# Where the twelve weight buffers and the moving operands of a float32r kernel start in their SBUF rows

## The chip, the core and the metric

The kernel runs on one core of a Trainium2 chip. The metric is the device time of one execution in microseconds (us). An interval between two matmuls is given in nanoseconds (ns).

## What is computed

Two transformer blocks work on one sequence of 256 tokens of width 1024, in float32. The first block mixes with gated spatial products, decaying ("forgetting") attention and attention on a memory, and ends in a feed-forward layer. The second block has two layers. Each is a gated feed-forward layer, an attention (sliding window in the first layer, latent attention in the second), and another gated feed-forward layer. Cut to what carries the time:

```python
f = jnp.square(jax.nn.relu(h @ w_ff1[l])) @ w_ff2[l]            # first block
...
def swiglu(h, wg, wu, wd):
    return (jax.nn.silu(h @ wg) * (h @ wu)) @ wd
...
x = x + 0.5 * swiglu(rmsnorm_2(x, ffn_norm1[i]), ffn1_wg[i], ffn1_wu[i], ffn1_wd[i])
x = x + sliding_window_attention(...)    # layer 0; latent_attention in layer 1
x = x + 0.5 * swiglu(rmsnorm_2(x, ffn_norm2[i]), ffn2_wg[i], ffn2_wu[i], ffn2_wd[i])
```

The feed-forward layers of the second block have 2816 inner columns, that of the first 4096. Each weight is read once; 208.71 MB are read from HBM in all.

## The kernel before

**Products in three passes.** A float32 product is made from float32r halves: every weight and every activation is split into a high part and a low part, and high·high, high·low and low·high are summed in PSUM. `mm_t` (lines 131 to 139) does this for one tile of the transposed result. The weight is the stationary operand (128 columns of it are loaded for each matmul), the activation the moving one (256 columns, the tokens):

```python
pe.matmul(ps, lhsT=h[:, c:c + m], rhs=x[0][k], start=s0, stop=False)     # line 137
pe.matmul(ps, lhsT=h[:, c:c + m], rhs=x[1][k], start=False, stop=False)  # line 138
pe.matmul(ps, lhsT=lo[:, c:c + m], rhs=x[0][k], start=False, stop=s1)    # line 139
```

`mm_n` (lines 141 to 149) makes the untransposed result of a few products: there the weight is the moving operand (256 to 512 columns) and the activation the stationary one.

**The weight stream.** The class `Stream` brings weights in transfers of up to 2048 columns into three `raw` buffers. It cuts each into parts of up to 1024 columns. For a part, ScalarE casts the high half into a `wh` buffer (line 100) and VectorE, in a few places GpSimd, subtracts it to get the low half in a `wl` buffer (line 110). There are six `wh` and six `wl` buffers, taken in turn, so twelve in all. A part of 1024 columns feeds 24 matmuls of `mm_t`. The order of the work is written out by hand (`manual_schedule`), engine by engine.

**The moving operands.** `xh` and `xl` (lines 154 and 155) are the halves of the normed input, eight tiles each. They are the moving operand of all projections from the input of a layer: queries, keys, the gate and up products. `ah` and `al` are the halves of the inner activation of a feed-forward layer and move through the down products. `oh` and `ol` are those of the attention outputs, `mh` and `ml` those of the memory. Each such tile is 256 float32r columns, which is 1024 bytes of a row (the part of a tile that lies in one partition).

**Places in the row.** The pools are laid one behind the other in the order in which they are opened: constants (`cst`), weights (`wp`), residual and normed tiles (`res`), temporaries (`tp`, `sm`), then the pools of each stage. Each tile starts at a multiple of 32 bytes. The constants come to a length that is no multiple of 512, and so everything behind them up to the stage pools starts at the same odd place. In the built program, by first byte in the row:

| tiles | before | remainder by 512 | changed | remainder by 512 |
|---|---|---|---|---|
| `raw`, 3 buffers | 24,928 on | 352 | 17,536 on | 128 |
| `wh` | 49,504 to 69,984 | 352, all six | 42,112 on, every 8,256 | 128, 192, 256, 320, 384, 448 |
| `wl` | 74,080 to 94,560 | 352, all six | 46,240 on, every 8,256 | 160, 224, 288, 352, 416, 480 |
| `xh`, `xl` | 106,848 to 122,208 | 352 | 99,840 to 115,200 | 0 |
| `ah`, `al`, `oh`, `ol`, `mh`, `ml`, `ch`, `cl` | 138,240 and beyond | 0 | 138,752 and beyond | 0 |

The 128-column slices of a weight buffer that the matmuls load lie 512 bytes apart, so all slices of a buffer have the remainder of its start.

Of the kernel before, what the change touches and what calls it, by code (L numbers as in the profile page):

```python
# [9 lines left out]
F32 = mybir.dt.float32  # L10
F32R = mybir.dt.float32r
BF16 = mybir.dt.bfloat16
I32 = mybir.dt.int32
# [4 lines left out]
P = 128  # L18
T = 256
# [4 lines left out]
CHUNK_COLS = 2048  # L24
PART = 1024
DN_CUT = 6
GAINS = ["norm_pre_mix", "norm_post_mix", "norm_pre_ffn", "norm_post_ffn", "norm_mem"]
# [8 lines left out]
N_COLS = 101  # L36
# [14 lines left out]
def block_kernel(ctx: ExitStack, tc: tile.TileContext, a: dict, out: bass.AP, upto: int = 99):  # L51
    nc = tc.nc
    pool = lambda name, bufs, **kw: ctx.enter_context(tc.tile_pool(name=name, bufs=bufs, **kw))
    cst = pool("cst", 1)
    wp = pool("wp", 1)
    res = pool("res", 1)
    tp = pool("tp", 2)
    sm = pool("sm", 1)
    psp = pool("psp", 8, space=bass.MemoryType.PSUM)
# [3 lines left out]
    def bank():  # L63
        return psp.tile([P, 512], F32, tag="ps", name="ps")

    # weight stream -------------------------------------------------------
    order = []
    RAW, HL, AHEAD = 3, 6, 4

    class Stream:  # L70
        """Weights come in transfers of up to CHUNK_COLS columns, each cut into parts; a part is
        split into float32r halves whose sum is the float32 weight."""

# [17 lines left out]
        def split(self, eng=dve):  # L91
            i = self.ns
            while len(self.parts) <= i and self.nd < len(order):
                self.dma()
            if i >= len(self.parts):
                return False
            t, n, last = self.parts[i]
            h = wp.tile([P, PART], F32R, tag="wh", bufs=HL, name=f"wh{i}")
            lo = wp.tile([P, PART], F32R, tag="wl", bufs=HL, name=f"wl{i}")
            act.copy(h[:, :n], t)  # L100
            self.hl[i] = (h, lo)
            self.ns += 1
            self.low(eng)
            self.late = (lo[:, :n], t, h[:, :n], last)
            return True
# [18 lines left out]
        def fill(self):  # L124
            """As many parts as there is room for, the low part of the last still to come."""
            while self.ns < self.ng + HL and self.split(gp):
                pass

    ws = Stream()

    # products ------------------------------------------------------------
    def mm_t(ps, w, off, n, x, kts, first, last, m=P):
# [17 lines left out]

    # constants -----------------------------------------------------------
    ctx.enter_context(tc.manual_schedule())
# [3 lines left out]
    X = (xh, xl)  # L156
    cols = cst.tile([P, N_COLS], F32, name="cols")
    kon = cst.tile([P, 3 * P], F32, name="kon")
    kmask = cst.tile([P, 768], F32, name="kmask")
    rows = cst.tile([P, N_ROWS], F32, name="rows")  # L160
    posr = cst.tile([P, T], I32, name="posr")
    posc = cst.tile([P, 64], I32, name="posc")
    posn = cst.tile([P, 2], I32, name="posn")
    relb = cst.tile([P, 2, 16], F32, name="relb")
    mhalf = cst.tile([P, 32], F32, name="mhalf")
    gp.memset(mhalf, -0.5)
# [5 lines left out]
    def gcol(i, k):  # L172
        return cols[:, i * KT + k:i * KT + k + 1]
# [3 lines left out]

    # norms ---------------------------------------------------------------
    def rstd_pow(dst, src, n):
        gp.tensor_tensor(out=dst, in0=src, in1=mhalf[:, :n], op=ALU.pow)  # L180
# [61 lines left out]
    def prep(k, g, acc):  # L242
        """High part of a tile of the next normed input now, low part of the tile before."""
        act.activation(out=xh[k], in_=x[k], func=AF.Copy, scale=gcol(g, k))  # L244
        if acc is not None:
            add_sq(acc, k, x[k])
        prep_end()
        late.append((k, gcol(g, k)))
# [5 lines left out]

    # attention -----------------------------------------------------------
    def attn_exp(u):
# [68 lines left out]
    class Pipe:  # L325
        """Heads in flight: each step transposes the probabilities of the head two back, scores a
        new one, multiplies the values of the head three back, and goes on with the softmaxes."""

# [44 lines left out]

    # FFN of the second block ----------------------------------------------
    def ffn2(acc, gnext, extra=(), start=None, more=()):
# [52 lines left out]
    def out_proj_start(pipe, oh, ol, sets):  # L428
        """The first four tiles of an output projection, between the last steps of the heads."""
        ps, w, todo = [bank() for _ in range(4)], [], []  # L430
        seen = 0
        for ks in sets:
            for d in range(4):
                if not seen:
                    w.append(ws.get(max(0, HL - 2 - d)))
                mm_t(ps[d][:, :T], w[d], 0, P, (oh, ol), ks, not seen, False)
                pipe.done() or pipe.step()
            seen = 1
        while not pipe.done():
            pipe.step()  # L440
        return ps, w
# [28 lines left out]
    def y_evac(d, p, y, yacc, gi):  # L470
        """One tile of a post-normed sublayer: times its gain, and its squares."""
        if d == KT - 1:
            sq = tp.tile([P, T], F32, tag="sq", name="sq")
            act.activation(out=sq, in_=p, func=AF.Square)
        else:
            sq = None
            add_sq(yacc, d, p)
        act.activation(out=y[d], in_=p, func=AF.Copy, scale=gcol(gi, d))
        return sq

    # relative position bias: a threshold mask of the distances times the steps between buckets,
    # 8 groups of 4 keys a set, sets 0-3 for the first query tile
    rbd = cst.tile([P, 3, 64], BF16, name="rbd")

# [51 lines left out]

    # ======================================================================
    seq = [("w1f", 0, 4), ("w1q", 0, 6), ("w1k", 0, 2), ("w1m", 0, 1), ("w1v", 0, 2), ("w1u", 0, 3),
# [6 lines left out]
    for nm, i0, i1 in seq:  # L545
        for i in range(i0, i1):
            src = [a[nm][i, 0], a[nm][i, 1]] if len(a[nm].shape) == 4 else [a[nm][i]]
            for ap in src:
                n = ap.shape[-1]
                cut = cuts.get(nm) or ([DN_CUT * P, n] if nm.startswith("dn") else list(range(PART, n + 1, PART)))  # L550
                order.append((ap, cut))

# [1 line left out]
    warm_table(AF.Exp)  # L554
# [20 lines left out]
    with ExitStack() as es:  # L575
        mp = es.enter_context(tc.tile_pool(name="mix", bufs=1))
# [22 lines left out]

        # values and gates of the forgetting heads (natural)  # L600
        acc = new_acc()
# [16 lines left out]

        # queries and keys of the forgetting heads
        pq = [bank() for _ in range(3)]  # L620
# [98 lines left out]

        # queries of the memory heads, memory keys and values, with the forgetting heads in between  # L720
        for i in range(2):
# [22 lines left out]
        for tt in range(2):  # L744
            act.activation(out=vm[tt], in_=pv[tt][:, :T], func=AF.Copy, scale=rs_m[:, tt:tt + 1])
        # gating branch, with the memory heads in between
        pg = [bank(), bank()]
# [37 lines left out]
        for j in range(3):  # L785
# [10 lines left out]
            f = tp.tile([P, T], F32, tag="f", name="f")  # L796
            gp.tensor_tensor(out=f, in0=t, in1=uT[j], op=ALU.mult)
            split_plain(oh[j], ol[j], f)

        # output projection, post norm  # L800
        yacc = new_acc("macc")
# [18 lines left out]

# [1 line left out]
    with ExitStack() as es:  # L822
# [17 lines left out]
        for i in range(2):  # L840
            t = ft.tile([P, 2 * T], F32, tag="t", name="t")
            act.activation(out=t[:, :T], in_=p[i][:, :T], func=AF.Relu)
            f = ft.tile([P, 2 * T], F32, tag="f", name="f")
# [48 lines left out]

# [1 line left out]
    with ExitStack() as es:  # L894
# [34 lines left out]
        mp = es.enter_context(tc.tile_pool(name="swa", bufs=1))  # L929
# [7 lines left out]
        rq = mp.tile([P, KT, 2, 2], F32, name="rq")  # L937
        ga = mp.tile([P, 1], F32, name="ga")
        dve.scalar_tensor_tensor(out=ga, in0=cols[:, C_AQ:C_AQ + 1], scalar=0.125, in1=cols[:, C_AK:C_AK + 1],
# [91 lines left out]

# [1 line left out]
    tq = cst.tile([P, 2, 2, 32], F32, name="tq")  # L1033
    tk = cst.tile([P, 2, 2, 32], F32, name="tk")

# [32 lines left out]
    with ExitStack() as es:  # L1068
        mp = es.enter_context(tc.tile_pool(name="mla", bufs=1))
# [10 lines left out]
        ol = [mp.tile([P, T], F32R, name=f"ol{k}") for k in range(KT)]  # L1080
        gb = mp.tile([P, 1], F32, name="gb")
        rqb = mp.tile([P, 4, 2, 4], F32, name="rqb")
# [3 lines left out]
        warm_table(AF.Exp)  # L1086
        # latent projections, transposed: keys and values first
        w, w2 = ws.get(), ws.get()
# [230 lines left out]

# [1 line left out]
def _kp(w):  # L1321
# [136 lines left out]
```

## Time and profile before

| | |
|---|---|
| median of 3 runs | 1295.81 us (1295.09 to 1299.8) |
| span of the profiled execution | 1296.4 us (its own total is not recorded apart from the span) |
| TensorE matmul / weight load busy | 98% / 94% |
| VectorE / ScalarE / GpSimd busy | 65% / 51% / 15% |
| HBM read | 208.71 MB, 162 GB/s over the span |
| granted TensorE clock, mean | 0.989 |

Matmuls are pipelined: one shows a duration of 280 ns or so and the next starts long before it ends. What one costs is therefore the interval from its start to the start of the next, which the timeline and the counts of matmuls in a stretch show. "PE" rows are matmuls, "PEld" rows the loads of stationary operands; the load for the next matmul runs beside the current one.

### The profile page before, as it was taken

The page shows a single profiled execution, that of the slowest core. Times are in us where ns is not written, and L with a number is a line of the kernel's source. Part 1 is how long each engine was busy: PE and PEld are TensorE (multiplying, and loading weights), DVE is VectorE, ACT ScalarE, POOL GpSimd, SP SyncE. Part 2 cuts the span into 40 slices and gives each one's busy share as a digit, 9 for nine tenths or more (in the row PEclk, how much of TensorE's full clock was granted, in tenths as well). Part 3 has the DMA queues.
Part 4 walks back from the last instruction along what each step waited for, and adds up shares of the span by engine and source line. Part 5 has one row for each costly group of instructions (what it writes and reads, how often), then busy time and mean ns, then how long its engine had stood idle before and what let it go on. Part 6 is the DMA issues. An engine that isn't in the chain of part 4 may idle for free.

```text
span 1296.4 us, 24835 instructions
## 1 busy us (share of the span) xinstructions
PE 1270.1 (98%) x10316; PEld 1223.0 (94%) x10316; DVE 846.0 (65%) x1490; ACT 661.6 (51%) x1174; POOL 197.4 (15%) x192
## 2 busy tenths in 40 slices
PE   8999899999899999999999999999999999999998
PEld 7789899999799999977999999999999878999998
DVE  6886676654686666686766556666566786666553
ACT  5556455434344544565544444545444787444442
POOL 4424210110420001210300001100001451100000
PEclk9999899999899999999999999999999989999999
DMA  7534355565145545621555556545456412555453
GB/s 230 197 117 145 115 174 193 195 222 177 57 138 200 184 149 190 218 94 34 177 201 176 174 163 210 192 172 196 165 164 199 160 65 70 188 171 191 154 196 106
DMA packets 37265, 211.37 MB, mean 163 GB/s; under 512 B 4768, under 2 KB 8224, under 8 KB 18848
## 3 DMA queue, kind: packets, MB, share of 16 engines
q1 hardware_dynamic: 37152, 209.78, 47.8%
q8 instruction: 81, 1.33, 0.4%
q14 instruction: 32, 0.26, 0.1%
HBM read 208.71 MB, written 1.05 MB: 162 GB/s over the span
## 4 chain that ended last, share of the span: by engine, by line
PE 88%; DVE 7%; issue 2%; DMA 1%; ACT 1%; POOL 0%; SPq 0%; ACTq 0%; DVEq 0%; POOLq 0%
PE ps L137 26%; PE ps L138 26%; PE ps L139 26%; DVE wl L110 3%; PE ps L289 2%; PE ps L315 2%; PE ps L300 1%; PE ps L147 1%; PE ps L148 1%; PE ps L149 1%; DMA raw<-in_w1k 1%; PE ps L317 1%; DMA raw<-in_w1f 0%; DVE dg L226 0%; ACT wh L100 0%
## 5 line engine op out<-in xcount | busy, mean ns | idle before, releaser
L137 PE MATMUL ps<-xh,wh 128*128 128x256 f32 (+1 forms) x1848 | 529.6, 287 | 1.6 <-ACT xh L525 1.6
L138 PE MATMUL ps<-xl,wh 128*128 128x256 f32 (+1 forms) x1848 | 527.1, 285 | 1.4 <-DVE xl L532 0.9
L139 PE MATMUL ps<-xh,wl 128*128 128x256 f32 (+1 forms) x1848 | 525.7, 284 | 2.0 <-DVE wl L110 2.0
L110 DVE TENSOR_TENSOR wl<-raw,wh 128x1024 fp32r<-128x1024 f32 (+3 forms) x434 | 489.3, 1166 | 48.1 <-ACT wh L100 46.5
L100 ACT CAST wh<-raw 128x1024 fp32r<-128x1024 f32 (+4 forms) x436 | 400.2, 957 | 67.0 <-PE ps L138 28.6
L137 PEld LDWEIGHTS ps<-xh,wh 128*128 128x128 f32 (+1 forms) x1848 | 356.6, 193 | 5.3 <-issue 3.2
L138 PEld LDWEIGHTS ps<-xl,wh 128*128 128x128 f32 (+1 forms) x1848 | 356.5, 193 | 3.4 <-DVE xl L532 2.3
L139 PEld LDWEIGHTS ps<-xh,wl 128*128 128x128 f32 (+1 forms) x1848 | 356.8, 193 | 2.2 <-DVE wl L110 2.2
L137 PE MATMUL ps<-ah,wh 128*128 128x256 f32 x960 | 268.6, 280 | 0.0
L138 PE MATMUL ps<-al,wh 128*128 128x256 f32 x960 | 268.6, 280 | 0.0
L139 PE MATMUL ps<-ah,wl 128*128 128x256 f32 x960 | 268.5, 280 | 0.0
L137 PEld LDWEIGHTS ps<-ah,wh 128*128 128x128 f32 x960 | 180.5, 188 | 0.0
L138 PEld LDWEIGHTS ps<-al,wh 128*128 128x128 f32 x960 | 180.5, 188 | 0.0
L139 PEld LDWEIGHTS ps<-ah,wl 128*128 128x128 f32 x960 | 180.5, 188 | 0.0
L385 ACT ACTIVATE s<-t 128x256 f32<-128x256 f32 x88 | 36.8, 418 | 204.3 <-DVE t L383 204.3
L191 POOL TENSOR_TENSOR acc<-acc,sq 128x256 f32<-128x256 f32 x42 | 49.9, 1188 | 598.2 <-ACT sq L190 598.1
L383 DVE TENSOR_TENSOR t<-ps,rb 128x256 f32<-128x256 f32 x88 | 37.2, 423 | 85.4 <-PE ps L139 79.9
L205 DVE TENSOR_TENSOR al<-f,ah 128x256 fp32r<-128x256 f32 (+1 forms) x105 | 48.9, 466 | 52.8 <-ACT ah L204 52.8
L204 ACT CAST ah<-f 128x256 fp32r<-128x256 f32 (+1 forms) x105 | 45.9, 437 | 55.7 <-DVE f L387 43.1
L244 ACT ACTIVATE xh<-x,cols 128x256 fp32r<-128x256 f32 x40 | 20.4, 510 | 101.8 <-DVE x L420 94.7
L387 DVE TENSOR_TENSOR f<-ps,s 128x256 f32<-128x256 f32 x88 | 37.3, 424 | 47.4 <-ACT s L385 47.4
L419 DVE SCALAR_TENSOR_TENSOR t<-ps,rb 128x256 f32<-128x256 f32 x32 | 13.6, 424 | 77.1 <-PE ps L139 77.1
(285 smaller groups left out, 1322.8 us busy)
## 6 DMA issues: line engine op xcount, KB each, us to landing
raw<-in_gu SPq DMA_DIRECT2D x88, 1024.0 KB, 5.0
raw<-in_dn SPq DMA_DIRECT2D x64, 704.0 KB, 4.3
raw<-in_ff SPq DMA_DIRECT2D x32, 1024.0 KB, 4.9
raw<-in_w_out SPq DMA_DIRECT2D x4, 1024.0 KB, 4.9
raw<-in_aq SPq DMA_DIRECT2D x4, 1024.0 KB, 5.0
raw<-in_a_out SPq DMA_DIRECT2D x4, 1024.0 KB, 4.8
raw<-in_b_out SPq DMA_DIRECT2D x4, 1024.0 KB, 4.9
raw<-in_w1q SPq DMA_DIRECT2D x6, 512.0 KB, 3.9
```

The costliest lines, as they stand in the source:

```text
L100: act.copy(h[:, :n], t)
L110: eng.tensor_tensor(out=lo, in0=t, in1=h.bitcast(F32), op=ALU.subtract)
L137: pe.matmul(ps, lhsT=h[:, c:c + m], rhs=x[0][k], start=s0, stop=False)
L138: pe.matmul(ps, lhsT=h[:, c:c + m], rhs=x[1][k], start=False, stop=False)
L139: pe.matmul(ps, lhsT=lo[:, c:c + m], rhs=x[0][k], start=False, stop=s1)
L191: gp.tensor_tensor(out=acc, in0=acc, in1=sq, op=ALU.add)
L204: act.copy(h, src)
L205: dve.tensor_tensor(out=lo, in0=src, in1=h.bitcast(F32), op=ALU.subtract)
L289: pe.matmul(ps[:, o:o + n], lhsT=u["q"][:, i * P:i * P + P], rhs=u["k"][:, :n], start=True, stop=True)
L383: dve.tensor_tensor(out=t, in0=g, in1=rb, op=ALU.mult)
L385: act.activation(out=s, in_=t, func=AF.Silu)
L387: dve.tensor_tensor(out=f, in0=u, in1=s, op=ALU.mult)
```

## The change

The weight buffers get a tag of their own each, so that they are laid out `wh0, wl0, wh1, wl1, ...`, and each is 8 columns (32 bytes) longer than the 1024 that are used. A part still goes to buffer `i % HL`, the sixth part after it to the same one. The pools are reordered and a filler tile is added in such a way that `xh` and `xl`, and all pools behind, start at multiples of 512 bytes. Two 1-column tiles (`ga`, `gb`) become 32 columns wide with only the first used, and the rope tables `tq`, `tk` are placed with the other constants. The instructions of each engine, their order, their shapes and what each waits for are the same in both programs; only addresses differ.

```diff
+STAGGER = 8
...
-    cst = pool("cst", 1)
+    lead = pool("lead", 1)
     wp = pool("wp", 1)
     res = pool("res", 1)
     tp = pool("tp", 2)
+    cst = pool("cst", 1)
     sm = pool("sm", 1)
...
-            h = wp.tile([P, PART], F32R, tag="wh", bufs=HL, name=f"wh{i}")
-            lo = wp.tile([P, PART], F32R, tag="wl", bufs=HL, name=f"wl{i}")
+            h = wp.tile([P, PART + STAGGER], F32R, tag=f"wh{i % HL}", name=f"wh{i}")
+            lo = wp.tile([P, PART + STAGGER], F32R, tag=f"wl{i % HL}", name=f"wl{i}")
             act.copy(h[:, :n], t)
...
+    lead.tile([P, 32], F32, name="fill")
+    mhalf = lead.tile([P, 32], F32, name="mhalf")
+    rbd = lead.tile([P, 3, 64], BF16, name="rbd")
+    relb = lead.tile([P, 2, 16], F32, name="relb")
+    posc = lead.tile([P, 64], I32, name="posc")
     kon = cst.tile([P, 3 * P], F32, name="kon")
     kmask = cst.tile([P, 768], F32, name="kmask")
+    posr = cst.tile([P, T], I32, name="posr")
+    tq = cst.tile([P, 2, 2, 32], F32, name="tq")
+    tk = cst.tile([P, 2, 2, 32], F32, name="tk")
+    cols = cst.tile([P, N_COLS], F32, name="cols")
...
-        ga = mp.tile([P, 1], F32, name="ga")
+        ga = mp.tile([P, 32], F32, name="ga")[:, 0:1]
...
-        gb = mp.tile([P, 1], F32, name="gb")
+        gb = mp.tile([P, 32], F32, name="gb")[:, 0:1]
```

## Rows read from the trace of the kernel before

**Rows 1.** Page: span, busy time of each engine, granted clock in 40 slices.

```profile
span 1296.4 us, 24835 instructions
PE 1270.1 (98%) x10316; PEld 1223.0 (94%) x10316; DVE 846.0 (65%) x1490; ACT 661.6 (51%) x1174; POOL 197.4 (15%) x192
...
PEclk9999899999899999999999999999999989999999
```

**Rows 2.** Page: chain that ended last, share by engine.

```profile
PE 88%; DVE 7%; issue 2%; DMA 1%; ACT 1%; POOL 0%; SPq 0%; ACTq 0%; DVEq 0%; POOLq 0%
```

**Rows 3.** Groups by line: engine, operation, names, shapes, count | busy us, mean ns | idle before.

```profile
L138 PE MATMUL ps<-xl,wh 128*128 128x256 f32 (+1 forms) x1848 | 527.1, 285 | 1.4 <-DVE xl L532 0.9 <-DVE xl L253 0.5
L138 PE MATMUL ps<-al,wh 128*128 128x256 f32 x960 | 268.6, 280 | 0.0
L138 PE MATMUL ps<-ol,wh 128*128 128x256 f32 x192 | 53.8, 280 | 0.0
L138 PE MATMUL ps<-ml,wh 128*128 128x256 f32 x16 | 4.5, 280 | 0.0
L138 PEld LDWEIGHTS ps<-xl,wh 128*128 128x128 f32 (+1 forms) x1848 | 356.5, 193 | 3.4 <-DVE xl L532 2.3 <-DVE xl L253 0.9
L138 PEld LDWEIGHTS ps<-al,wh 128*128 128x128 f32 x960 | 180.5, 188 | 0.0
```

**Rows 4.** Timeline of PE, x products (640 us): start us, us, engine, line, operation.

```profile
640.07 0.28 PE L139 MATMUL ps<-xh,wl 128*128 128x256 f32 x1
...
676.07 0.28 PE L139 MATMUL ps<-xh,wl 128*128 128x256 f32 x1
```

**Rows 5.** Timeline of PE, down products (960 us).

```profile
960.04 0.28 PE L137 MATMUL ps<-ah,wh 128*128 128x256 f32 x1
...
995.24 0.28 PE L137 MATMUL ps<-ah,wh 128*128 128x256 f32 x1
```

**Rows 6.** Stretches: us, busy (count) of PE, PEld, DVE, ACT, POOL, clock, DMA.

```profile
640.00:680.00 40.00, 40.00 (x335) 40.00 (x335) 25.98 (x39) 19.90 (x30) 0.00 (x0) 1.00 0.51 168
960.00:1000.00 40.00, 40.00 (x343) 40.00 (x342) 26.15 (x37) 18.92 (x33) 6.04 (x5) 1.00 0.58 189
541.00:612.00 71.00, 71.00 (x479) 56.82 (x479) 49.82 (x180) 43.32 (x135) 10.68 (x10) 1.00 0.24 86
```

**Rows 7.** Timeline of PE, memory values (65 us): moving weight, stationary memory tile.

```profile
65.19 0.28 PE L147 MATMUL ps<-wh,mh 128*128 128x256 f32 x1
...
67.35 0.28 PE L147 MATMUL ps<-wh,mh 128*128 128x256 f32 x1
```

**Rows 8.** Timeline of PE, latent projection (1008 us): stationary loads of 32 columns.

```profile
1008.78 0.28 PE L138 MATMUL ps<-xl,wh 128*32 128x256 f32 x1
...
1010.48 0.28 PE L138 MATMUL ps<-xl,wh 128*32 128x256 f32 x1
```

**Rows 9.** Timeline of PE, 384 moving columns, stationary xh (90 us).

```profile
90.65 0.33 PE L147 MATMUL ps<-wh,xh 128*128 128x384 f32 x1
...
91.69 0.33 PE L147 MATMUL ps<-wh,xh 128*128 128x384 f32 x1
```

**Rows 10.** Timeline of PE, 384 moving columns, stationary ch (1022 us).

```profile
1022.59 0.34 PE L147 MATMUL ps<-wh,ch 128*128 128x384 f32 x1
...
1023.65 0.34 PE L147 MATMUL ps<-wh,ch 128*128 128x384 f32 x1
```

**Rows 11.** Weight stream: the cast, the subtraction, the landing of a transfer, SyncE's waits.

```profile
L110 DVE TENSOR_TENSOR wl<-raw,wh 128x1024 fp32r<-128x1024 f32 (+3 forms) x434 | 489.3, 1166 | 48.1 <-ACT wh L100 46.5 <-PE ps L138 1.1
L100 ACT CAST wh<-raw 128x1024 fp32r<-128x1024 f32 (+4 forms) x436 | 400.2, 957 | 67.0 <-PE ps L138 28.6 <-DMA raw<-in_dn 15.8 <-DMA raw<-in_w1q 7.1
raw<-in_gu SPq DMA_DIRECT2D x88, 1024.0 KB, 5.0
SPq L86 <- DVE wl L110: 984.9, 202, 22.3
```

More of the change, by code (lines that the diff above doesn't have):

```diff
@@ L156, in block_kernel @@
     X = (xh, xl)
-    cols = cst.tile([P, N_COLS], F32, name="cols")
+    lead.tile([P, 32], F32, name="fill")
[3 more added lines that the diff above has]
+    posc = lead.tile([P, 64], I32, name="posc")
     kon = cst.tile([P, 3 * P], F32, name="kon")
     kmask = cst.tile([P, 768], F32, name="kmask")
+    posr = cst.tile([P, T], I32, name="posr")
+    tq = cst.tile([P, 2, 2, 32], F32, name="tq")
+    tk = cst.tile([P, 2, 2, 32], F32, name="tk")
+    cols = cst.tile([P, N_COLS], F32, name="cols")
     rows = cst.tile([P, N_ROWS], F32, name="rows")
-    posr = cst.tile([P, T], I32, name="posr")
-    posc = cst.tile([P, 64], I32, name="posc")
     posn = cst.tile([P, 2], I32, name="posn")
-    relb = cst.tile([P, 2, 16], F32, name="relb")
-    mhalf = cst.tile([P, 32], F32, name="mhalf")
     gp.memset(mhalf, -0.5)
@@ L479, in y_evac @@
         return sq
-    rbd = cst.tile([P, 3, 64], BF16, name="rbd")
     def rel_parts():
@@ L1030, in block_kernel @@
         return dump()
-    tq = cst.tile([P, 2, 2, 32], F32, name="tq")
-    tk = cst.tile([P, 2, 2, 32], F32, name="tk")
     def rope_tables():
```

## The prediction

> **What bounds the kernel now.** The page's first lines come first: TensorE has a matmul in flight for 1270.1 us of the span of 1296.4 us and loads weights for 1223.0 us, VectorE follows with 846.0 us, and the granted clock is full (a 9 in the row of 40 slices means 90% or more) in 37 of the 40 slices [rows 1]. [...] The chain that ended last is 88% TensorE [rows 2]. So the time is the number of matmuls times the interval at which they start, and whatever changes that interval changes the total almost one for one.
>
> The groups by line give the numbers. Each of the three passes of `mm_t` has 1848 matmuls with xh or xl as moving operand, and 960 + 192 + 16 = 1168 with ah, oh, mh or their low halves [rows 3], of which one pass is shown. Times three: 5544 and 3504. All have 256 moving columns, and nearly all load 128 stationary ones.
>
> Then the timeline, where the point of this case lies. Among the x products, the 301st start comes 36.00 us after the first, so the interval is 120.0 ns [rows 4]. Among the down products 300 intervals take 35.20 us, so 117.33 ns [rows 5]. The counts of matmuls in 40 us say the same, 335 against 343, with clock 1.00 and without a pause of TensorE in both stretches [rows 6]. Same instruction, shape and clock; the weight loads also differ, 193 against 188 ns [rows 3]. What differs by the table of places is the moving operand: xh and xl start 352 bytes past a multiple of 512, ah, oh and mh on one. The weights start at 352 in both.
>
> Three smaller places tell more. With the weight moving (at 352) and a memory tile stationary (at 0), 18 intervals take 2.16 us: 120.0 ns again [rows 7]. So moving at 352 costs 120.0 whether the stationary operand starts equally (x products) or 160 bytes further on. At 384 moving columns an equal start gives 173.3 ns, one 160 further 176.7 [rows 9, 10]: being apart is no gain in itself. And with stationary loads of only 32 columns, 15 intervals take 1.70 us, 113.3 ns, with moving still at 352 [rows 8]. So part of the interval hangs on the load that runs beside the matmul.
>
> **The change part by part.** Order, shapes and waits are the same on every engine, so there is nothing to count but addresses. Two things happen to them.
>
> *Moving operands to multiples of 512.* 5544 matmuls get a moving operand of the kind that the 3504 have now. The nearest row is 117.33 ns [rows 5]: 5544 x (120.0 - 117.33) = 14.8 us. I take off 0.8 us, because 8 x 24 = 192 of them stand between the heads of the sliding-window stage, where the loads are busy only 56.8 of 71 us [rows 6], and others at the start of layers, where TensorE waits for the normed tiles; there an earlier end waits too. That leaves 14.0.
>
> *The stagger.* With moving at 0, the only stationary start that the trace shows is 352, which after the change one buffer of twelve has (`wl3`). The other eleven start at 128 to 480 in steps of 32. No row shows them. Bounds for their interval are 113.3 ns (the shorter loads, rows 8), and 120.0 ns (all that moving at 352 costs, rows 4 and 7). I take 117.33 for all of them, since it is the one row with the moving operand where it will be, and it holds alike for ah, oh and mh: then the 3504 stay as they are and the stagger costs nothing.
>
> *The rest.* The 200-odd matmuls of `mm_n` have the weight moving, now at twelve different starts. Rows 9 and 10 differ by 3.4 ns, so 96 products of 384 or 390 columns against stationary x tiles cost at most 0.3 us more, which I leave out. Casts and subtractions write at other addresses; one part feeds 24 matmuls, 24 x 117.33 = 2.82 us, and takes 0.957 us of ScalarE and 1.166 us of VectorE [rows 11], so even a tenth more there stays hidden (the work that hides it is those 24 matmuls). A transfer of 1024 KB lands in 5.0 us, feeds 48 matmuls or 5.63 us, and SyncE waits 984.9 us in all for a free buffer [rows 11]: the stream runs ahead of its use and still does at 2% more speed. Buffers are freed in the same order, six parts later. Next late after TensorE would be VectorE at 26 of 40 us [rows 6], far off.
>
> **Sum:** 1296.4 - 14.0 = 1282.4 against the span; the median of the runs is 0.6 us lower than that span, so 1281.8, said as **1282 us**.
>
> [...] The trace shows two intervals for one shape at one clock [rows 4, 5]. [...]
>
> **Rivals.**
>
> *No effect.* The x tiles and all weight buffers lie below byte 123,232 of the row, the ah, oh and mh tiles beyond 138,240; that remains so after the change. If moving and stationary data in one region cost 120.0 ns and in two 117.33, the same rows come out, and rows 7 too if it only matters where the moving operand lies. Then nothing moves: 1296. For it: rows 4, 5 and 7 can't separate region from remainder. Against it: the weight buffers spread over 49 KB, and yet all x products keep one interval to the 0.1 ns over 300 starts, which a remainder common to all explains more simply.
>
> *Slower, by the stagger.* In the present kernel the 3504 meet their weights at one start, 352, and it may be a favourable one. If the other eleven starts cost 120.0, then x gains only on one buffer in twelve, 5544 x 2.67 / 12 = 1.2 us, and the 3504 lose 3504 x 2.67 x 11/12 = 8.6 us: 1296.4 + 7.4 = 1303.8, so 1303 by the median. It is decided by the mean interval over the twelve starts: no change at (5544 x 120.0 + 3504 x 117.33) / 9048 = 118.97 ns. A measurement of this kernel can tell some 0.5%, 6.5 us, from no change, which is 0.72 ns of that mean: faster below 118.25, slower above 119.69. For it: distance does matter at 384 columns [rows 9, 10], and 352 was not chosen. Against it: 120.0 has been seen only with moving at 352.
>
> *Cheaper starts.* If collisions of load and moving operand become rarer than at 352, the mean lies below 117.33. At 115.0, midway to rows 8, the gain is 5544 x 5.0 + 3504 x 2.33 = 35.9 us: 1260. At 113.3 it is 5544 x 6.7 + 3504 x 4.03 = 51 us: 1245. For it: short loads show that the interval can be that low with 256 columns moving. Against it: those loads are a quarter as long, and no row with 128 stationary columns comes down to it.
>
> **How the numbers follow.** The forecast, a mean between 116.3 and 118.2 ns (gains of 5544 x 3.7 + 3504 x 1.03 = 24 us down to 5544 x 1.8 - 3504 x 0.87 = 7 us, so 1272 to 1289), has 0.48. No effect has 0.18, cheaper starts 0.22, slower 0.12. Faster is the forecast and the cheaper starts, 0.70; same is 0.18; slower 0.12. The range takes the forecast, no effect, and the nearer part of the cheaper starts (0.14 of 0.22), 0.80 in all: 1260 to 1297.
>
> **What would show it.** Right: in the timeline of the gate and up products 300 intervals take about 35.2 us instead of 36.0, a 40 us stretch of them counts about 343 matmuls, and their weight loads come to about 188 ns; the down products keep 117.3, whichever buffer they use. Wrong by no effect: x stays at 120.0 and its loads at 193 ns. Wrong by the stagger: the interval changes from buffer to buffer, every 24 matmuls, with groups at or above 120 among the down products. Wrong by cheaper starts: intervals below 117 in both. Busy times of VectorE, ScalarE and DMA should not change in any case.

## The result, and the profile after

The changed kernel takes 1287.94 us (median of 5 runs, 1287.19 to 1288.61), the kernel before 1295.81 us (median of 5, 1295.09 to 1300.19). The ratio is 0.9932, with a 95% interval of 0.9914 to 0.995: faster by 0.5 to 0.9%. 1282 us had been forecast, with a range of 1260 to 1297. The profiled execution of the changed kernel is one of those runs: 1287.94 us, with a span of 1286.1 us, so 1.84 us lie outside the span. The prediction set the span of before against the median as if the two were the same measure; they are not: by about the same difference the profiled execution of before (span 1296.4 us) took some 1298 us. The sum is not changed by it, since 1295.81 - 14.0 gives the same 1281.8.

The page's lines that answer to [rows 1] and [rows 2] (span, busy time of each engine, granted clock in 40 slices, chain that ended last):

```profile
span 1286.1 us, 24835 instructions
...
PE 1261.6 (98%) x10316; PEld 1213.8 (94%) x10316; DVE 846.1 (66%) x1490; ACT 663.0 (52%) x1174; POOL 197.2 (15%) x192
...
PEclk9999899999799999999999999999999999999999
...
PE 88%; DVE 6%; issue 2%; ACT 2%; DMA 1%; POOL 0%; SPq 0%; ACTq 0%; POOLq 0%; DVEq 0%
```

TensorE lost 8.5 us of matmul time and 9.2 us of weight loading; VectorE and GpSimd changed by 0.2 us at most, ScalarE by 1.4 us. The groups by line, as in [rows 3] (lines have moved by two: 138 is now 140):

```profile
L140 PE MATMUL ps<-xl,wh 128*128 128x256 f32 (+1 forms) x1848 | 521.5, 282 | 1.3 <-DVE xl L538 0.8 <-DVE xl L261 0.5
L140 PE MATMUL ps<-al,wh 128*128 128x256 f32 x960 | 268.8, 280 | 0.0
L140 PEld LDWEIGHTS ps<-xl,wh 128*128 128x128 f32 (+1 forms) x1848 | 349.3, 189 | 3.3 <-DVE xl L538 2.2 <-DVE xl L261 0.9
L140 PEld LDWEIGHTS ps<-al,wh 128*128 128x128 f32 x960 | 180.5, 188 | 0.0
```

The loads beside the x products went from 193 to 189 ns, those beside the down products stayed at 188. The timelines, as in [rows 4] and [rows 5], each from one start to the 301st, first x products, then down products:

```profile
640.05 0.28 PE L139 MATMUL ps<-xh,wh 128*128 128x256 f32 x1
...
675.46 0.28 PE L139 MATMUL ps<-xh,wh 128*128 128x256 f32 x1
...
960.00 0.28 PE L141 MATMUL ps<-ah,wl 128*128 128x256 f32 x1
...
995.32 0.28 PE L141 MATMUL ps<-ah,wl 128*128 128x256 f32 x1
```

300 intervals of the x products take 35.41 us, 118.0 ns each (36.00 us before); 300 of the down products 35.32 us, 117.7 ns (35.20 before). The stretches say the same, 341 matmuls where there were 335 and 342 where there were 343 [rows 6] (columns: us; busy and count of PE, PEld, DVE, ACT, POOL; clock; DMA share; GB/s):

```profile
640.00:680.00 40.00, 40.00 (x341) 40.00 (x341) 27.00 (x38) 20.65 (x30) 0.00 (x0) 1.00 0.56 187
960.00:1000.00 40.00, 40.00 (x342) 40.00 (x341) 26.08 (x38) 19.14 (x32) 6.71 (x5) 1.00 0.59 199
```

So x gained, but less than forecast, and the down products lost a little. The interval also changes from buffer to buffer, the sign that the prediction named for its rival of the stagger, though without groups at 120 among the down products. These are the first matmuls of seven parts of 24, one after the other, in the gate and up products; by the built program the first part lies in buffer 3 (starts 320 and 352), then come 4, 5, 0, 1, 2 and 3 again:

```profile
851.09 0.28 PE L139 MATMUL ps<-xh,wh 128*128 128x256 f32 x1
...
853.95 0.28 PE L139 MATMUL ps<-xh,wh 128*128 128x256 f32 x1
...
856.77 0.28 PE L139 MATMUL ps<-xh,wh 128*128 128x256 f32 x1
...
859.60 0.28 PE L139 MATMUL ps<-xh,wh 128*128 128x256 f32 x1
...
862.43 0.28 PE L139 MATMUL ps<-xh,wh 128*128 128x256 f32 x1
...
865.25 0.28 PE L139 MATMUL ps<-xh,wh 128*128 128x256 f32 x1
...
868.09 0.28 PE L139 MATMUL ps<-xh,wh 128*128 128x256 f32 x1
```

Buffer 3 takes 2.86 us (119.2 ns), buffers 4 and 1 take 2.82 (117.5), 5 and 0 2.83 (117.9), 2 takes 2.84 (118.3). No buffer is at 120.0, none much below 117.3.

For the rest of this text the intervals are means over whole traces: all intervals between two float32r matmuls of 256 moving columns with loads of 128 columns, without a pause, at granted clock 1.00. They come from one profiled execution of each kernel. There are about 5390 of them among the x products and 3469 among the products of a, o and m (called down products here). Before they are 119.93 and 117.43 ns, after 117.99 and 117.88.

### The profile page after: what moved, and what is told of

Same layout as the page of the kernel before. It is cut to its first block, busy times and chain, and to the rows that moved or that the text cites. A ratio compares the mean times of both kernels' runs of the same rounds, so it can differ in the third digit from the quotient of the medians.

```text
span 1286.1 us, 24835 instructions
## 1 busy us (share of the span) xinstructions
PE 1261.6 (98%) x10316; PEld 1213.8 (94%) x10316; DVE 846.1 (66%) x1490; ACT 663.0 (52%) x1174; POOL 197.2 (15%) x192
## 4 chain that ended last, share of the span: by engine, by line
PE 88%; DVE 6%; issue 2%; ACT 2%; DMA 1%; POOL 0%; SPq 0%; ACTq 0%; POOLq 0%; DVEq 0%
PE ps L139 26%; PE ps L140 26%; PE ps L141 26%; PE ps L297 2%; DVE wl L112 2%; PE ps L323 2%; PE ps L308 1%; PE ps L149 1%; PE ps L151 1%; PE ps L150 1%; ACT wh L102 1%; PE ps L325 1%; DMA raw<-in_w1q 1%; DVE dg L234 0%; DMA raw<-in_w1f 0%
## 5 line engine op out<-in xcount | busy, mean ns | idle before, releaser
L139 PE MATMUL ps<-xh,wh 128*128 128x256 f32 (+1 forms) x1848 | 523.2, 283 | 0.6 <-ACT xh L531 0.6
L140 PE MATMUL ps<-xl,wh 128*128 128x256 f32 (+1 forms) x1848 | 521.5, 282 | 1.3 <-DVE xl L538 0.8
L112 DVE TENSOR_TENSOR wl<-raw,wh 128x1024 fp32r<-128x1024 f32 (+3 forms) x434 | 489.3, 1167 | 45.9 <-ACT wh L102 45.4
L139 PEld LDWEIGHTS ps<-xh,wh 128*128 128x128 f32 (+1 forms) x1848 | 350.4, 190 | 4.4 <-issue 3.2
L140 PEld LDWEIGHTS ps<-xl,wh 128*128 128x128 f32 (+1 forms) x1848 | 349.3, 189 | 3.3 <-DVE xl L538 2.2
L141 PEld LDWEIGHTS ps<-xh,wl 128*128 128x128 f32 (+1 forms) x1848 | 349.3, 189 | 1.2 <-DVE wl L112 1.1
```

What stands on the lines that cost most here:

```text
L112: eng.tensor_tensor(out=lo, in0=t, in1=h.bitcast(F32), op=ALU.subtract)
```

## The experiments

All twelve kernels are the changed kernel with other starts; in the built programs only addresses differ. Five of the twelve were run once: the three maps of distances, the one with weights at 32, and the one with a single low half at 352. The pads are set by two lists, in columns of 4 bytes, and filler tiles keep everything behind at its old remainder unless said otherwise:

```diff
-STAGGER = 8
+PAD_H, PAD_L = (0, 0, 0, 0, 0, 0), (0, 0, 0, 0, 0, 0)
...
-            h = wp.tile([P, PART + STAGGER], F32R, tag=f"wh{i % HL}", name=f"wh{i}")
+            b = i % HL
+            if i < HL and PAD_H[b]:
+                wp.tile([P, PAD_H[b]], F32, tag=f"ph{b}", name=f"ph{b}")
+            h = wp.tile([P, PART], F32R, tag=f"wh{b}", name=f"wh{i}")
```

The same is done for `wl` with `PAD_L`. (Shortened: a second pair of lists, zero in every run, is left out of the tile's width, and so are the lines that open the pools `tail` and `ctl` of the filler tiles.) Below, "distance" is the start of the loaded buffer minus that of the moving tile, by the remainder by 512.

### The moving start alone

No stagger: x at 0 as in the change, all twelve buffers at 352.

```diff
-    lead.tile([P, 32], F32, name="fill")
+    lead.tile([P, 88], F32, name="fill")
+    tail.tile([P, 40], F32, name="tailpad")
```

> This is the change without its stagger: xh and xl at multiples of 512 as in the change, all twelve weight buffers 352 past one as in the kernel before. Theory A (the start of the moving operand made the gain, the stagger costs part of it): x products and down products both at 117.33 ns, so (5390 x (117.99 - 117.33) + 3469 x (117.88 - 117.33)) = 5.5 us less than the change, about 1282.5 us, and the weight loads at 188 ns. Theory B (the stagger made the gain, the start of the moving operand alone does nothing): x products back at 120.0 ns, about 1295 us. Theory C (the region of the row matters, not the remainder by 512): x stays at 120.0 as well.

Measured: 1289.33 us (1288.56 to 1293.9), ratio 0.9956 [0.9941, 0.997]; x 117.90, down 117.76 ns. The move alone takes x from 120 to nearly what the down products had, as the prediction thought, but the total comes down by 6.1 us, not by 14. Neither group comes to 117.33, and the down products, whose starts by 512 are those of before, got slower. The trace shows why: whole parts run at 117.3 ns (five intervals that repeat, 116, 120, 117, 115, 118) or at 118.7 (120, 116, 117, 119, 122), at one and the same distance. The slower kind has 66 of 177 down parts and 92 of 218 x parts here; in the kernel before it has 8 of 177 down parts. Such a repeating sequence is called a rhythm below. In the sum by intervals the move gives 5390 x 2.03 - 3469 x 0.33 = 9.8 us. Some of what is missing to that may be clock: the mean granted clock of its runs was 0.985 to 0.991 against 0.988 to 0.993 of before.

### The stagger alone

x back at 352, the twelve buffers staggered from 0 to 352 in steps of 32.

```diff
-    lead.tile([P, 32], F32, name="fill")
+    ctl.tile([P, 40], F32, name="ctailpad")
+PAD_H, PAD_L = (0, 8, 8, 8, 8, 8), (8, 8, 8, 8, 8, 8)
```

> The stagger alone: weight buffers 32 bytes further each, from 0 to 352, but xh and xl 352 past a multiple of 512 as in the kernel before (ah, oh, mh on multiples). Theory A: x products stay at 120.0 ns or near it, down products at 117.9 as in the change, so 1296 to 1298 us. Theory B (the stagger makes the gain): x products near 118.0, so about 1288 us.

Measured: 1287.75 us (1284.64 to 1288.9), ratio 0.9929 [0.9913, 0.9946]; x 117.91, down 118.15 ns. With the moving operand where it was in the kernel before, the stagger gives all that the change gives. So it is not the multiple of 512: either half of the change takes x away from the equal start of before, and the two do not add up.

### A map of distances

Moving operands at 0, both buffers of a pair at the same start, 32 further from pair to pair. Two kernels cover 0 to 160 and 192 to 352 (the pairs of starts that later expectations speak of).

```diff
+PAD_H, PAD_L = (0, 8, 8, 8, 8, 8), (0, 0, 0, 0, 0, 0)
-    lead.tile([P, 32], F32, name="fill")
```

```diff
+PAD_H, PAD_L = (0, 8, 8, 8, 8, 8), (0, 0, 0, 0, 0, 0)
-    lead.tile([P, 32], F32, name="fill")
+    lead.tile([P, 48], F32, name="fill")
```

> Moving operands at multiples of 512; high and low buffer of one part start alike, the six pairs at 0, 32, 64, 96, 128 and 160. It reads six starts at once, by the interval of the 24 matmuls of a part. Theory A: 117.33 ns for all six, also for the equal start 0. Theory D (an equal start of load and moving operand locks them at a worse interval): 120.0 ns at 0 and near 117.33 elsewhere. Theory E (each start has its own interval and 117.33 is only that of 352): values spread between 113 and 120, and the change's mean of 118 is their mean.

> As the run before it, with the six pairs at 192, 224, 256, 288, 320 and 352. Theory A: 117.33 ns for all. Theory E: a spread from 113 to 120, with 117.33 at 352. If all are alike here and in the run before, the excess of the change (118.0 against 117.33) comes from the 32 bytes between the high and the low buffer of a part, not from the starts.

Measured: 1290.41 us and 1281.61 us. The interval goes with the distance, and the x and the down products take the same values at each (table below): 113.9 ns at 192, about 120 at 0, 160 and 256. The timeline of the second map shows it in one run through the buffers, each line the first matmul of 24; the first part lies at 320, then come 352, 192, 224, 256, 288 and 320 again:

```profile
849.90 0.28 PE L146 MATMUL ps<-xh,wh 128*128 128x256 f32 x1
...
852.73 0.28 PE L146 MATMUL ps<-xh,wh 128*128 128x256 f32 x1
...
855.55 0.28 PE L146 MATMUL ps<-xh,wh 128*128 128x256 f32 x1
...
858.27 0.28 PE L146 MATMUL ps<-xh,wh 128*128 128x256 f32 x1
...
861.07 0.28 PE L146 MATMUL ps<-xh,wh 128*128 128x256 f32 x1
...
863.95 0.28 PE L146 MATMUL ps<-xh,wh 128*128 128x256 f32 x1
...
866.78 0.28 PE L146 MATMUL ps<-xh,wh 128*128 128x256 f32 x1
```

In us per part: 2.83 at 320, 2.82 at 352, 2.72 at 192 (113.3 ns), 2.80 at 224, 2.88 at 256 (120.0), 2.83 at 288.

A third kernel covers 384, 416, 448, 480, 480 and 0.

```diff
+PAD_H, PAD_L = (0, 8, 8, 8, 0, 8), (0, 0, 0, 0, 0, 0)
-    lead.tile([P, 32], F32, name="fill")
+    lead.tile([P, 96], F32, name="fill")
```

> A map of what is left: moving operands at multiples of 512, the pairs of weight buffers at 384, 416, 448, 480, 480 and 0. Theory E with a period of 256 bytes (0 and 256 gave 119.8, 32 and 288 gave 118.3): 384 as 128 (118.3 ns), 416 as 160 (120.0), 448 as 192 (113.9), 480 as 224 (116.8), 0 at 119.8; mean 117.6 and about 1284 us. With a period of 512 the pairs at 384 to 480 can be anything between 113.3 and 120.0, 1262 to 1303 us.

Measured: 1295.71 us, 12 us more than the sum with a period of 256 gave; 8 of them are intervals (a mean of 118.5 instead of 117.6 ns), the rest the sum by intervals doesn't account for. 384 and 416 came out as expected of it (118.4 and 119.9 ns), but 448 gave 117.7 where 192 had given 113.9. All distances of the three kernels, x and down products together:

| distance | ns | distance | ns |
|---|---|---|---|
| 0 | 119.7 | 256 | 119.7 |
| 32 | 118.3 | 288 | 118.3 |
| 64 | 113.3 to 114 or 117.8, by part | 320 | 113.3 to 114 or 117.8, by part |
| 96 | 117.3, 118.7 or 120, by part | 352 | 117.3, 118.7 or 120, by part |
| 128 | 118.4 | 384 | 118.4 |
| 160 | 120.0 | 416 | 119.9 |
| 192 | 113.9 | 448 | 117.7 |
| 224 | 116.8 | 480 | 117.7 |

The two columns agree but in the last two rows. And at 64, 96, 320 and 352 whole parts run at one of two or three values: a sign that a distance alone does not settle it.

### Distance, or where the bytes lie

All starts at 0, moving and loaded: the kernel that by the prediction should have been the fastest.

```diff
-    lead.tile([P, 32], F32, name="fill")
+    tail.tile([P, 128], F32, name="tailpad")
```

> All moving operands and all twelve weight buffers start at multiples of 512 bytes, no stagger. Theory E: the worst distance, 0, now for the down products too, so x stays at 120.0 ns as in the kernel before and the down products go from 117.4 to 120.0: 3469 x 2.5 = 9 us slower than the kernel before, 1304 us. The theory of the prediction (a moving operand at a multiple of 512 gives 117.33 whatever the load's start): x goes to 117.33, 1282 us. Rival F: no two buffers differ in the kernel before nor here, so 1296 or less.

Measured: 1304.68 us (1304.14 to 1304.93), ratio 1.0069 [1.0053, 1.0084], slower than before. The down products, whose moving operand did not move, went from 117.43 to 119.96 ns (343 matmuls in the stretch of [rows 6], now 336); x stayed at 119.93:

```profile
640.00:680.00 40.00, 40.00 (x334) 39.94 (x333) 25.77 (x40) 20.27 (x31) 0.00 (x0) 1.00 0.46 159
960.00:1000.00 40.00, 40.00 (x336) 40.00 (x335) 25.30 (x36) 18.31 (x31) 6.06 (x5) 1.00 0.56 183
```

This falls on the forecast of distance 0 to the microsecond (1304). It also ends the rival of the regions: x and a tiles lie in different regions of the row here and cost the same (119.93 and 119.96 ns). And distance 0 costs 119.93 ns with both starts at 352 (x, before) and with both at 0.

In the next kernel x lies at 352 and the weights at 32: distance 192 for x, 32 for the down products.

```diff
-    lead.tile([P, 32], F32, name="fill")
+    lead.tile([P, 8], F32, name="fill")
+    tail.tile([P, 80], F32, name="tailpad")
+    ctl.tile([P, 40], F32, name="ctailpad")
```

> Weight buffers all at 32 past a multiple of 512, xh and xl at 352 past one, the other moving operands at a multiple. The distance from moving to load is 192 for the x products (modulo 512) and 32 for the down products. Theory E by distance: x at about 113.9 ns, the down products at about 118.3; 5390 x (117.99 - 113.9) = 22 us less than the changed kernel for x and 1 us more for the rest, so 1267 us. If it is the absolute start of the load that sets the interval: both at about 118.3 and 1290 us. If it is the absolute start of the moving operand: x at 120.0 and 1296 us or more.

Measured: 1287.25 us; x 117.68, down 118.32 ns. The down products are as the map has 32. x is not at 113.9, the one value the forecast had, but neither at the 118.3 of a load at 32 nor at 120. Its intervals are a repeating 117, 118, 118 with a few at 113 and 114, which is what distance 192 also does in the next run. With 0 and 192, two distances were thus seen at other starts too; for the rest of the map no run shows that the distance counts and not the start of the load.

### All at the best distance

```diff
-    lead.tile([P, 32], F32, name="fill")
+    lead.tile([P, 48], F32, name="fill")
+    tail.tile([P, 80], F32, name="tailpad")
```

> All moving operands start at multiples of 512 bytes, all twelve weight buffers at 192 past one, with no stagger. Theory E (the interval belongs to the distance from the start of the moving operand to that of the stationary load, each distance having its own, which the two looks at pairs of starts gave): every x and every down product at about 113.9 ns, as the two buffers at 192 had among their neighbours; against the changed kernel 5390 x 4.1 + 3469 x 4.0 = 36 us less, so 1252 us. Rival F (what counts is that neighbouring buffers differ, so the short interval at 192 hung on the buffer before or after it): without a stagger it falls back to 117.3 to 120.0, and the time to 1283 to 1297 us.

Measured: 1285.44 us (1282.1 to 1286.34), ratio 0.9914 [0.9899, 0.9929]: not 1252. x 117.33, down 117.52 ns on average, but this is a mixture. Two stretches of the one trace:

```profile
160.00:200.00 40.00, 40.00 (x355) 40.00 (x355) 31.44 (x32) 25.14 (x36) 5.76 (x7) 1.00 0.54 189
640.00:680.00 40.00, 40.00 (x342) 40.00 (x341) 26.45 (x37) 20.07 (x30) 0.00 (x0) 1.00 0.55 189
```

Same matmuls, same addresses, same clock: 355 in 40 us here, 342 there. In the first stretch the starts repeat 113, 113, 114 ns (113.3), in the second 117, 118, 118, 118, 117, 119 and the like (117.8). One unbroken run of 113 and 114 is 547 matmuls long (from 143.9 us of the span), one of the other kind 1556, and both end where matmuls of another shape come between. So this distance has two lasting rhythms, and what a stretch does depends on how it is entered. Behind a pause or other matmuls it is mostly the longer one, in 30 of the 32 stretches of more than a dozen matmuls.

### What makes the rhythm

In the second map the buffer at 192 came behind one at 352, and 60 of 64 such entries without a pause ended in 113.3 ns (the expectations say 62, without two that came from 118.7 ns). So one pair at 352 was put among five at 192, and in a second kernel only its low half.

```diff
+PAD_H, PAD_L = (0, 0, 0, 0, 0, 40), (0, 0, 0, 0, 0, 0)
-    lead.tile([P, 32], F32, name="fill")
+    lead.tile([P, 48], F32, name="fill")
+    tail.tile([P, 40], F32, name="tailpad")
```

> Moving operands at multiples of 512, buffers 0 to 4 (high and low) at 192 past one, buffer 5 at 352. Theory G (at one distance there are several lasting rhythms, and the one in which a stretch goes is set by the rhythm that it comes from: at 192 one of 113.3 ns, entered from a buffer at 352 in 60 of 62 cases of the look at pairs, and one of 117.3, entered after a pause of TensorE, in which the kernel with all buffers at 192 spent nearly all its time): each pass over buffer 5 puts the next five buffers into 113.3 until the next pause; 0.81 of their parts at 113.4, the rest at 117.4, buffer 5 at 118.3, mean 114.9 instead of 117.4, 8856 x 2.5 = 22 us less than with all at 192: 1263 us, 1255 to 1268. Rival H (only the first buffer behind the one at 352 is short, the rhythm is not kept): one buffer in six at 113.4, mean 117.0, 1282 us. Rival I (the short interval hung on something else of that look, the other starts or how the parts fell): no gain, 1286 us.

> As the kernel before it, but of buffer 5 only the low half at 352, the high half at 192: the load alternates between the two starts inside that part, every third matmul. Theory G: the step from 352 to 192 is what starts the rhythm of 113.3, and the last matmul of the part loads at 352, so the next five buffers are short here too, and the part itself mixes: 1256 to 1266 us. If a whole stretch at 352 is needed for it, the buffers stay at 117.3: 1285 us.

(The second has the 40 in `PAD_L`.) Measured: 1286.7 us (1286.18 to 1291.15), ratio 0.9926 [0.9911, 0.9941], and 1279.93 us in the one run of the second. The first is a miss: 192 stayed at 117.6 ns. Three starts of its timeline, the first matmul of the part at 352, of the five parts at 192, and of the next at 352:

```profile
859.67 0.28 PE L146 MATMUL ps<-xh,wh 128*128 128x256 f32 x1
...
862.49 0.28 PE L146 MATMUL ps<-xh,wh 128*128 128x256 f32 x1
...
876.62 0.28 PE L146 MATMUL ps<-xh,wh 128*128 128x256 f32 x1
```

24 intervals take 2.82 us (117.5 ns), the next 120 take 14.13 us (117.8 ns). A buffer at 352 leads back to the longer rhythm of 192 here, in 62 of 64 entries without a pause between. It was itself entered from that rhythm nearly always, and it is not in one state: of its 65 parts 30 run at 117.3 ns, 34 at 118.7 and one at 120.0. In the second kernel about a fifth of the intervals are at 113 or 114, also far from the forecast.

So the step before is not enough: what 352 passes on depends on what it was entered from. In the second map that had been a buffer at 320. The last two kernels bring this chain back, the one with 320 and 352 behind four pairs at 192, the other with 288, 320 and 352 behind three.

```diff
+PAD_H, PAD_L = (0, 0, 0, 0, 32, 8), (0, 0, 0, 0, 0, 0)
-    lead.tile([P, 32], F32, name="fill")
+    lead.tile([P, 48], F32, name="fill")
+    tail.tile([P, 40], F32, name="tailpad")
```

(The other has `PAD_H` 0, 0, 0, 24, 8, 8.)

> Moving operands at multiples of 512, buffers 0 to 3 (high and low) at 192 past one, buffer 4 at 320, buffer 5 at 352. Theory J (the rhythm a buffer falls into depends on the point of its cycle at which the stretch before it ends, so more than one step back counts; in the look at pairs the chain 320, 352, 192 ended in 113.3 ns whichever of its two rhythms 320 had, in 60 of 62 cases, while 352 entered from 192 led back to 117.3): four buffers of six at 113.4 but for the part before the first pass after a pause, 0.81 of them, the rest at 117.4, 320 at 116.5, 352 at 118.3; mean 115.2 instead of the 117.4 of all at 192, 8856 x 2.2 = 20 us less: 1266 us. If the chain needs 288 ahead of 320 to work, 192 stays at 117.4 and the time is 1284 to 1288 us.

> As the kernel before it, with buffer 3 at 288 too: the chain of the look at pairs from 288 on, word for word the same distances. Theory J: three buffers of six at 113.4 (0.81 of their parts, the rest at 117.4), 288 at 118.3, 320 at 116.5, 352 at 118.3, mean 115.9, 8856 x 1.5 = 13 us less than with all at 192: 1272 us. If the rhythm goes back further still than 288 (256 or 224 ahead of it), 192 falls to 117.4 and the time is about 1288 us.

Measured: **1263.21 us** (1261.98 to 1264.8), ratio 0.9747 [0.9731, 0.9762], and 1273.2 us (1271.57 to 1273.88), ratio 0.9826 [0.9811, 0.984]: 3 and 1 us from the forecasts. The sizes of single buffers were not as forecast (in the first, 113.3 instead of 116.5 ns at 320 and 120.0 instead of 118.3 at 352), and in the second only 46 of 64 entries from 352 into 192 ended in 113.3 ns. The first beats both kernels, the changed one by some 24 us (the quotient of the ratios, 0.9747 / 0.9932, is 0.981). From its page, and one stretch:

```profile
span 1260.2 us, 24835 instructions
...
PE 1234.2 (98%) x10316; PEld 1186.8 (94%) x10316; DVE 845.6 (67%) x1490; ACT 660.3 (52%) x1174; POOL 197.7 (16%) x192
```

```profile
640.00:680.00 40.00, 40.00 (x352) 40.00 (x351) 25.56 (x37) 19.10 (x28) 0.00 (x0) 1.00 0.57 192
```

And one round of its six pairs in the timeline: the part at 352, the four at 192, that at 320, 352 again:

```profile
840.19 0.28 PE L146 MATMUL ps<-xh,wh 128*128 128x256 f32 x1
...
843.08 0.28 PE L146 MATMUL ps<-xh,wh 128*128 128x256 f32 x1
...
853.96 0.28 PE L146 MATMUL ps<-xh,wh 128*128 128x256 f32 x1
...
856.68 0.28 PE L146 MATMUL ps<-xh,wh 128*128 128x256 f32 x1
...
859.56 0.28 PE L146 MATMUL ps<-xh,wh 128*128 128x256 f32 x1
```

24 intervals of 120.4 ns by these rows (2.89 us), 96 of 113.3 (10.88 us), 24 of 113.3 (2.72 us), 24 of 120.0 (2.88 us). A round keeps itself going: over all runs with such steps, 320 entered from 192 at 113.3 runs at 113.3 as well (52 of 52), 352 entered from that runs at 120.0, its longer rhythm (102 of 102), and 192 entered from 352 at 120.0 runs at 113.3 (110 of 110). One expensive part pays for five cheap ones. What decides the entries from 352 at 117.3 ns is told at the end of the section on the prediction.

### All runs beside the sum

The intervals of each run, and what they give for the total: (119.93 - x) times about 5390 plus (117.43 - down) times 3469, against the difference of the medians (for the five kernels run once, of that one time) from the kernel before on the same chip.

| kernel | x ns | down ns | sum, us | measured, us |
|---|---|---|---|---|
| the change | 117.99 | 117.88 | -8.9 | -7.9 |
| moving start alone | 117.90 | 117.76 | -9.8 | -6.1 |
| stagger alone | 117.91 | 118.15 | -8.4 | -7.7 |
| pairs 0 to 160 | 118.50 | 118.43 | -4.2 | -5.1 |
| pairs 192 to 352 | 117.30 | 117.13 | -15.2 | -13.9 |
| pairs 384 to 480, 0 | 118.54 | 118.53 | -3.7 | +0.3 |
| all 0 | 119.93 | 119.96 | +8.8 | +9.3 |
| weights 32, x 352 | 117.68 | 118.32 | -9.0 | -8.1 |
| all 192 | 117.33 | 117.52 | -13.7 | -10.0 |
| 192, one pair 352 | 117.66 | 117.64 | -11.5 | -9.2 |
| 192, one low half 352 | 116.85 | 116.98 | -18.2 | -16.0 |
| 192 four times, 320, 352 | 115.22 | 114.81 | -34.5 | -33.9 |
| 192 three times, 288, 320, 352 | 115.82 | 116.59 | -25.1 | -23.9 |

The intervals carry the result in every kernel, to 4 us at worst and to 2.3 us in ten of thirteen. The rest may go with differences of the granted clock between runs (before, in the first series: 0.993 in runs of 1294.4 us, 0.988 in runs of 1297.6 to 1298.2) and with the single profile that each row of intervals is from.

## Why the prediction was right, and where it was not

**What bounds the kernel: right.** The time is the number of matmuls times their interval. The table above bears it out in thirteen kernels, to 4 us at worst.

**The x term: right in direction, too large.** Forecast 5544 x 2.67 = 14.8 us, less 0.8; the trace of after gives 5390 x 1.94 = 10.5 us, because x went to 117.99 and not to 117.33.

**The stagger at nothing: wrong by a small cost.** The down products went from 117.43 to 117.88 ns: 3469 x 0.45 = 1.6 us. Together -8.9 instead of -14.0 us, and -7.9 by the medians; the two terms are most of the difference to the forecast.

**The step that failed** is the reading of rows 4, 5 and 7: that moving at 352 costs 120.0 and moving at 0 costs 117.33, whatever the load's start (the second half was taken for eleven starts that no row showed). Rows 4 and 7 looked like one cause because both had the moving operand at 352, and both show 120.0 ns at granted clock 1.00. By distance they are two cases, 0 in rows 4 and -352, which is 160 by the remainder, in rows 7, and the map has 120 for both. Rows 5 are distance 352. The kernel with everything at 0 shows it without a doubt: by the forecast's reading it would take 1282 us, it takes 1304.68. The kernel with the stagger alone shows the other side: moving at 352 and yet 117.91. That the change helped is not the gain of a good place but the loss of a bad one: x sat at one of the most expensive distances (0, at 119.93 ns), and a spread over twelve distances brings it near their mean of some 118, as one other distance, 352, does on average. The text had the point of no change at 118.97 ns for that mean, and it came out at (5390 x 117.99 + 3469 x 117.88) / 8859 = 117.95, inside the 116.3 to 118.2 of the forecast. That it fell inside is luck: 117.33 was the faster rhythm of a single distance, which only one of the twelve buffers keeps, and the mean of the other starts happened to lie close to it.

**No effect: refuted.** Same instructions in the same order at 1304.68 and 1263.21 us, by addresses alone. The regions of the row play no part that shows: the x and the down products take the same values at each distance (119.93 and 119.96 ns at 0). The intervals moved with the time: x is at 119.93 ns in the one, at 115.22 in the other.

**Slower by the stagger: half right.** There are starts at 120 (0, 160, 256 and 416), as that rival held possible, but they are four of sixteen, besides some parts at 96 and 352. It named 352 a favourable start for the down products; at 117.43 it was a little better than the mean of 118. In the change high and low alternate between two distances, and the parts of its six buffers came out at 117.5 to 118.9 ns, so the price that the rival named, 120, was not paid.

**Cheaper starts: there are such intervals, but not in this change.** Intervals of 113.3 exist with 128-column loads, for up to 547 matmuls in a row, against the reason given (only 32-column loads had shown them). The change passes 192 too, but with high at 192 and low at 224 the load alternates between two distances, and that part came out at about 117.6 ns. Whether collisions of load and moving operand set the interval was not shown by any run.

**The rest at nothing: right.** Busy times of VectorE 846.0 and 846.1 us, of ScalarE 661.6 and 663.0. The cast, the subtraction and SyncE's main wait, as in [rows 11]:

```profile
L112 DVE TENSOR_TENSOR wl<-raw,wh 128x1024 fp32r<-128x1024 f32 (+3 forms) x434 | 489.3, 1167 | 45.9 <-ACT wh L102 45.4
L102 ACT CAST wh<-raw 128x1024 fp32r<-128x1024 f32 (+4 forms) x436 | 401.1, 959 | 62.0 <-PE ps L140 30.8 <-DMA raw<-in_dn 13.7 <-DMA raw<-in_w1q 7.6
SPq L88 <- DVE wl L112: 977.3, 202, 22.9
```

1166 and 1167 ns, 957 and 959 ns, and 977 us of waiting instead of 985: the stream still runs ahead. The kernel at 1263 us leaves it 953 us.

**What decides between two rhythms at the entry.** It isn't the mean interval of the stretch before: 352 at 117 to 117.5 ns led to 113.3 ns at 192 in 43 of 45 cases in the second map and in 1 of 29 with one pair at 352. By the starts in the traces it is the point of its cycle at which the part at 352 ends, as theory J had it. Of the 107 such entries without a pause (the second map, the kernel with one pair at 352, and the last two):

| last intervals of the part at 352, ns | 192 runs at 113.3 | 192 runs at 117.8 |
|---|---|---|
| 120, then 116 or 117 | 18 | 0 |
| 120, then 116 or 117, then 115 | 42 | 0 |
| 115, then 118 or 119 | 0 | 10 |
| 118 or 119, then 116 or 117 | 0 | 18 |
| 116 or 117, then 120 | 0 | 19 |

Both outcomes occur within one kernel (43 and 2, 1 and 28, 8 and 1, 8 and 16), always by this point. Entries from 352 in its rhythm of 120.0 ended in 113.3 ns in 110 of 110 cases, those from its rhythm of 118.7 in 117.8 in 39 of 39. The step from 288 into 320 shows the same: a part at 288 that ended on an interval of 120 led to 113.3 ns in 48 of 48 entries, one that ended on 121 to 123 to 117.8 in 27 of 27.

**What stays open.** This was read from the traces afterwards; no run set that point alone. Why the point, and the distance itself, change the interval isn't shown by any run either.

## What to carry to other kernels

Where a kernel runs at the rate of its matmuls, compare the start-to-start interval of equal matmuls between its stages. Where it has two values for one shape and clock, as 119.93 and 117.43 ns here, look for what else differs; here it was addresses, so they belong on the list. Vary one start at a time and note the distance between the loaded and the moving operand, not only the remainder of one of them. And look at the sequence of intervals, not at their mean alone: where it repeats in two patterns, the order in which buffers follow each other can be worth as much as the choice of one start (here 22 us between all buffers at 192 and the same with the last two at 320 and 352, and 19 us between all at 0 and all at 192).

## What was not expected of the hardware

- The interval of a 256-column float32r matmul with a 128-column load, at clock 1.00 and as a mean over a part, lay between 113.3 and 120.0 ns in these kernels, by the distance of the two starts and by the rhythm, and in the map a distance and the one 256 bytes further agreed in six of eight cases. Of the exceptions, 192 showed the 117.8 of 448 too in a later run, and three short stretches at 448 (5 to 10 intervals) ran at 113 and 114.
- At 192 two lasting rhythms were seen, 113.3 and 117.8 ns, kept over up to 547 and 1556 matmuls in a row. At 320 they were 113.3 and 117.8, at 352 there were three, 117.3, 118.7 and 120.0.
- In the changed kernel, where the loads inside a part alternate between starts 32 bytes apart (high and low), the interval up to a matmul whose load lies 32 bytes back was longer than that up to one whose load lies 32 further: 119.3 against 116.8 ns at 192 and 224. The step back also goes on to the next 128 columns of the weights and the next moving tile, and no run separates the two.
- The kernel with all buffers at 192 varied by 4.2 us between runs (1282.1 to 1286.34), that with all at 0, which has one rhythm, by 0.8. Only one execution of each was profiled, so that the runs of the first differ in their rhythms was not seen.
